# Own tiles for the last gate stores, the division in the score banks, and an output projection interleaved by row blocks

## The chip, the cores and the metric

The kernel runs on one core of a Trainium2 chip. The metric is the device time of one execution in microseconds (us); lower is better. A core has five instruction queues that run side by side and each in its own order: PE (TensorE, the matmuls), ACT (ScalarE), DVE (VectorE), POOL (GpSimd) and SP, which only issues DMAs here. An instruction that waits holds up everything behind it on its own queue.

## What is computed

The reference is one layer of a decoder: 1024 tokens and 16 learned meta tokens ahead of them, width 1024.

```python
h = rms_norm(h_res, pre_norm_g[i])
z = h @ w_in[i]                                   # 1024 -> 7328 columns
(pv, pg, cq, ckv, kr, mg, cu, cg, sbcx, sg, gl) = split_cols(z)
y_a = (pool_mixer(pv, ...) * silu(pg)) @ w_out_pool[i]
y_b = (mla_attention(cq, ckv, kr, ...) * silu(mg)) @ w_out_mla[i]     # 8 heads, causal
y_c = (conformer_conv(cu, ...) * silu(cg)) @ w_out_conf[i]
y_d = (short_conv(sbcx, ...) * silu(sg)) @ w_out_sc[i]
gts = sigmoid(gl + gate_bias[i]).reshape(b_, l_, 4, D_MODEL)
m = gts[:, :, 0] * y_a + gts[:, :, 1] * y_b + gts[:, :, 2] * y_c + gts[:, :, 3] * y_d
h_res = h_res + rms_norm(m @ w_o[i], post_norm_g[i])
return h_res[:, N_META:]
```

## The kernel before, in words

**Arithmetic.** Every large product is made of three matmuls: each fp32 operand is split into a rounded part and the rest (`split`: a copy on ACT, then a subtraction on POOL or DVE), and hi times hi, hi times lo and lo times hi are summed in PSUM. A matmul of 128 rows and 512 columns is the usual unit.

**Order of the work.** No instruction is written where it runs. The program's text records instructions (`Plan.record`), and `Plan.flush` plays them through a model: every instruction has a cost and becomes ready when what it depends on has ended, and each free engine takes the ready one of the lowest priority number. That order is then issued. `plan.ahead(n)` lowers the priority numbers, `plan.behind()` makes an instruction wait for the last matmul recorded. Tiles live in pools with a number of slots per tag; a tile of a tag gets the next slot that comes free, and two pools of different stages may lie over the same bytes. The real waits between engines and DMAs are semaphores put in afterwards from the true data dependences.

**Stage 1: input projection.** `unit` multiplies a 256-column pair of weight blocks with the normalised tokens by a seven-product scheme (A11, A12, A22 and the sums S1 to S4 of weight blocks against B11, B21, T1 to T4 and B22 of token blocks). It works in PSUM banks `ps_pa` to `ps_pd`, and calls `out(i, j, ...)` for the four 128 x 512 results in the order (1,1), (1,0), (0,0), (0,1). For the gates, `out_gate` adds on DVE, takes a tanh on ACT into a tile `z`, and stores it to DRAM (`th_dram`). The `z` tiles come from a tag with three slots (`halves_of`). Stores are issued on ACT's queue, and for the last pair of gates (g == 30) on POOL's. The seven split weight blocks of a pair are tiles of the tag `blk`, seven slots.

**Stage 2: attention.** For 8 heads and 2 halves of the queries, `attend` makes scores in PSUM (`ps_s`, tag `s`, five banks, taken as they come free), exponentiates them on ACT, splits the result (`pt`: ACT, then POOL) and multiplies with the values into `ps_o`. `maxima` runs ahead for the row maxima of the next unit and writes them into extra rows of the query tile `qt`. Between the units, `fills` computes the output products of the other three branches into `ps_y` (tag `y`, two banks): 48 products of six matmuls, each followed on DVE by a gate multiplication (`th`), and for the second and third of these branches by an addition into `m`: on POOL for the second, on DVE for the third. The division by the softmax sum goes through DRAM (`sums`) for the first seven heads, and for the last head through PE (`sums_pe`): four transposes of the sums, a reciprocal `lcp` on DVE, four transposes back, in two banks of the tag `y`.

**Stage 3: output projection.** First eight steps of the attention's own output product (`ps_u`), then `m @ w_o` by the same seven products, on 128-row blocks t = 0 to 3: `product(ps, b, name, t, ...)` is 12 matmuls (4 slices k of the weight, 3 each). The weights are loaded raw (`wr`, three slots) on SP's queue, four slices for each of the seven names, and split into tiles `wa` (ten slots), the low part on POOL for even k and on DVE for odd k. Row block t gives rows t and t + 4 of the output, four 512-column quarters: `c11` and `a_` for t, `u2` and `c22` for t + 4. Each quarter is squared on ACT with a running sum (`square`), multiplied by the norm's gain on POOL (`gain`), and `final(t, ...)` makes the reciprocal root (DVE, then a power on POOL, `rso`), scales and adds the residual rows `xr` on DVE (`scalar_tensor_tensor`) and stores on SP's queue. The last three products run in turn over all row blocks: S1 for t = 0..3 (`c22`), S4 for t = 0..3 (`u2`, rows t + 4 are finished), A22 for t = 0..3 (`a_`, rows t are finished). The last A22 product is done in two halves of 256 columns.

Of the kernel before, what the change touches and what calls it, by code (L numbers as in the profile page):

```python
# [21 lines left out]
F32 = mybir.dt.float32  # L22
# [8 lines left out]
P = 128  # L31
# [183 lines left out]
class Plan:  # L215
# [8 lines left out]
    def __init__(self, nc):  # L224
        self.nc, self.ops, self.todo, self.lift, self.pipe = nc, [], [], 0, None
        self.pools, self.past, self.extra, self.landed, self.wait = [], [], 0, [], None
# [57 lines left out]

    @contextmanager
    def slow(self, ns):

        self.extra += ns
        yield
        self.extra -= ns  # L290
# [26 lines left out]
    def record(self, eng, op, args, kw):  # L317
# [4 lines left out]
        if kw.get("accum_out") is not None:  # L322
# [4 lines left out]
            isinstance(v, View) and v.buf.psum for v in outs + ins)  # L327
        o = {"i": len(self.ops), "turns": turns, "prio": len(self.ops) - self.lift, "eng": eng, "op": op, "args": args, "kw": kw,
             "cost": cost, "bytes": nbytes, "extra": 0 if getattr(getattr(outs[0], "buf", None), "dram", True) else self.extra, "bufs": set(), "deps": set() if self.wait is None else {self.wait}, "users": [], "end": None}
# [26 lines left out]
    def flush(self):  # L356
# [38 lines left out]
        while events:  # L395
# [11 lines left out]
            for e in self.free:  # L407
# [21 lines left out]
                self.free[e] = t + o["cost"]  # L429
                o["end"] = t + o["cost"] + self.WAKE[e]  # L430
                if o["op"] == "dma_start":
# [28 lines left out]
def trunk_kernel(ctx, tc, a):  # L460
# [285 lines left out]
    def out_gate(g):  # L746

        def each(i, to, ps, x, tmp):
            if x is not None:
                full(to, x, ps)  # L750
            ACT.activation(to, ps if x is None else to, AF.Tanh, scale=0.5,
                           bias=par[:, R_GB + g + i:R_GB + g + i + 1])
        return halves_of(512, each, lambda i, j, t: (POOL if g == 30 else ACT).dma_start(half(th_dram[g + i], j), t))

# [746 lines left out]
    def sums_pe(h, c):  # L1501

        pc = bank("y")[:, :256].rearrange("p (j n) -> p j n", n=64)
        for j in range(4):
            PE.transpose(pc[:, j].in_order(), ol[h][64:, c, P * j:P * (j + 1)], ident[64:, 64:])
        lc = at.tile([P, 4], F32, tag="lcp", bufs=2, name="lcp")
        DVE.reciprocal(lc, pc[:, :, 0])
        rb = bank("y")[:64]
        for j in range(4):
            PE.transpose(rb[:, P * j:P * (j + 1)], lc[:, j:j + 1].to_broadcast([P, 64]), ident)  # L1510
        return rb
# [22 lines left out]
    def fills():  # L1534
# [9 lines left out]
        for bi, (gi, wname, b0) in enumerate(branches):  # L1544
            bo = [bos[bi, k] for k in range(2)]
            for d in range(KD):
# [8 lines left out]
                for c in range(2):  # L1555
# [128 lines left out]
    def weights(name):  # L1684

        for k in range(KH):
# [56 lines left out]

    def gain(src, i, out=None, c0=0):

        n = src.shape[1]
        mul(POOL, src if out is None else out, src, pgB[:, 512 * i + c0:512 * i + c0 + n])

    AHEAD = 60

    def final(t, h0, h1):

        rs_ = slice(P * t, P * (t + 1))
        with plan.ahead(AHEAD):
            DVE.tensor_reduce(rso[:, t:t + 1], sso[:, t], axis=AX.X, op=ALU.add)

            rsqrt_mean(rso[:, t:t + 1], rso[:, t:t + 1], D, 16 * EPS)
        for i, h in enumerate((h0, h1)):
            s_ = slice(512 * i, 512 * (i + 1))
# [38 lines left out]
    for t in range(4):  # L1798
        po[t], c22[t] = bank("o"), half("c22")
# [4 lines left out]
    for t in range(4):  # L1804
        product(po[t], B22, "S4", t, False, True)
        add(DVE, u2[t], po[t], u2[t])
        square(t + 4, 0, u2[t])
        gain(u2[t], 0)
        final(t + 4, u2[t], c22[t])
    for t in range(4):  # L1810

        parts = [slice(0, 512)] if t < 3 else [slice(0, 256), slice(256, 512)]
        g = half("g", 1) if t == 3 else a_[t]
        for i, cols in enumerate(parts):
# [4 lines left out]
            square(t, 1 + i, a_[t][:, cols])  # L1819
            gain(a_[t][:, cols], 1, g[:, cols], cols.start)  # L1820
        final(t, c11[t], g)
    plan.hold(kept, -1)
# [36 lines left out]
```

## Time and profile before

| | us |
|---|---|
| runs | 983.56, 987.5, 989.2 (median 987.5) |
| the profiled execution, its own time | 983.37 |
| its span, first to last instruction | 981.2 |
| PE busy in the span | 961.4 (98%) |
| DVE, POOL, ACT busy | 689.3, 679.2, 449.1 |
| mean granted TensorE clock | 0.991 |

Between the span and the execution's own time lie 2.2 us. In the trace all instructions of the body have the line L354, since the plan issues all of them there; so they are told apart by tile names (`ps_s<-qt,kt`: a score product) and by time. Stage 1 runs to 641.2 us, stage 2 to 851.6, stage 3 to the end. In a timeline row the first number is the start and the second the duration, "x12" counts merged instructions, and the bracket at the end gives the idle time of that engine just before and what ended it. PEq, ACTq and the like are an engine's queue; a row "SPq ... DMA" is the issue of a DMA, not its transfer.

### The profile page before, as it was taken

Reading aid. Unit: us, or ns where it says so; the run is one execution under the profiler, and the core shown is the slowest. Engines: PE = TensorE matmul, PEld = TensorE weight load, DVE = VectorE, ACT = ScalarE, POOL = GpSimd, SP = SyncE. Lnnn points to the kernel's source line nnn. Section 1 sums busy time; section 2 is a strip of 40 time slices with the busy share of each in tenths; the row PEclk is TensorE's granted clock in tenths of the full one; section 3 lists DMA queues with packets and bytes.
Section 4 is the critical chain, followed back from the end, with each engine's and each line's share of the span. In section 5 each row is a group of like instructions: output and inputs, shape, how many; then the busy total and the mean of one; then the engine's idle time right before and its main releaser. Section 6 shows DMA issues by size and latency. Waiting matters only on the chain.

```text
span 981.2 us, 15371 instructions
## 1 busy us (share of the span) xinstructions
PE 961.4 (98%) x5063; PEld 819.9 (84%) x5063; DVE 689.3 (70%) x1109; ACT 449.1 (46%) x914; POOL 679.2 (69%) x632
## 2 busy tenths in 40 slices
PE   9999999999999999999999999979999999999996
PEld 9999899889888888888788888868788888788885
DVE  6946968968969965445554777236867778699747
ACT  7644333343343554544443444356465565224631
POOL 6747645666677797877687789346387896546956
PEclk9999999999999999999999999979999999999998
DMA  7146567667686687675746788679859764772534
GB/s 255 35 114 174 154 223 231 199 213 255 195 279 232 200 260 213 220 245 181 210 153 191 235 292 279 174 238 330 224 165 289 196 196 130 257 253 92 188 123 172
DMA packets 136295, 202.76 MB, mean 207 GB/s; under 512 B 20814, under 2 KB 83253, under 8 KB 135448
## 3 DMA queue, kind: packets, MB, share of 16 engines
q1 hardware_dynamic: 127240, 185.00, 60.9%
q10 hardware_dynamic: 8656, 15.74, 4.4%
q0 software_dynamic: 320, 1.05, 0.3%
q8 instruction: 40, 0.66, 0.3%
q14 instruction: 39, 0.32, 0.1%
HBM read 128.86 MB, written 72.88 MB: 206 GB/s over the span
## 4 chain that ended last, share of the span: by engine, by line
PE 91%; DVE 4%; DMA 3%; issue 1%; ACT 1%; SPq 0%; POOL 0%; DVEq 0%; POOLq 0%; ACTq 0%
PE ps_pb L354 16%; PE ps_pa L354 16%; PE ps_pc L354 15%; PE ps_o L354 9%; PE ps_pd L354 7%; PE ps_u L354 7%; PE ps_s L354 7%; PE ps_y L354 6%; PE ps_x L354 5%; PE ps_w L354 1%; DMA th<-z 1%; DMA kt<-k 1%; DMA vt<-v 1%; DVE th L354 1%; DVE a L354 1%
## 5 line engine op out<-in xcount | busy, mean ns | idle before, releaser
L354 PE MATMUL ps_pb<-T,S 128*128 128x512 f32 (+2 forms) x792 | 172.4, 360 | 0.0
L354 PE MATMUL ps_pa<-B,A 128*128 128x512 f32 (+2 forms) x792 | 169.4, 359 | 0.0
L354 POOL TENSOR_TENSOR S<-ss,S 128x512 fp32r<-128x512 f32 x84 | 114.0, 1369 | 62.1 <-ACT S L354 61.9
L354 PEld LDWEIGHTS ps_pa<-B,A 128*128 128x128 f32 x792 | 134.3, 188 | 22.5 <-issue 0.7
L354 PEld LDWEIGHTS ps_pb<-T,S 128*128 128x128 f32 x792 | 134.1, 189 | 22.4 <-issue 1.0
L354 POOL TENSOR_TENSOR A<-raw,A 128x512 fp32r<-128x512 f32 x84 | 114.7, 1371 | 43.4 <-ACT A L354 37.0
L354 POOL TENSOR_TENSOR pt<-p,pt 128x512 fp32r<-128x512 f32 (+1 forms) x96 | 101.5, 1080 | 44.1 <-PE ps_s L354 22.7
L354 DVE TENSOR_TENSOR u<-ps_pb,u 128x512 f32<-128x512 f32 (+2 forms) x66 | 40.2, 610 | 80.6 <-PE ps_pb L354 76.7
L354 DVE SCALAR_TENSOR_TENSOR ps_w<-conv,par,ps_w 128x512 f32<-128x512 f32 x116 | 87.2, 752 | 2.3
L354 ACT ACTIVATE S<-ss 128x512 fp32r<-128x512 f32 x84 | 50.8, 628 | 81.5 <-DVE ss L354 50.1
L354 PE MATMUL ps_pc<-B,S 128*128 128x512 f32 (+1 forms) x396 | 86.2, 360 | 0.0
L354 PE MATMUL ps_pd<-T,A 128*128 128x512 f32 (+2 forms) x396 | 85.4, 359 | 0.0
L354 PE MATMUL ps_y<-bo,whl 128*128 128x512 f32 x288 | 85.1, 404 | 0.2 <-DVE th L354 0.2
L354 PE MATMUL ps_pc<-T,S 128*128 128x512 f32 (+1 forms) x396 | 85.0, 358 | 0.0
L354 PEld LDWEIGHTS ps_pc<-B,S 128*128 128x128 f32 x396 | 66.9, 189 | 11.7 <-issue 1.2
L354 PEld LDWEIGHTS ps_pc<-T,S 128*128 128x128 f32 x396 | 66.9, 189 | 10.7
L354 ACT ACTIVATE p<-ps_s 128x512 f32<-128x512 f32 (+4 forms) x112 | 49.4, 442 | 57.8 <-PE ps_s L354 31.3
L354 PE MATMUL ps_s<-qt,kt 100*128 100x512 f32 (+4 forms) x336 | 70.8, 334 | 5.1 <-DVE qt L354 5.1
L354 PEld LDWEIGHTS ps_pd<-T,A 128*128 128x128 f32 x396 | 66.9, 189 | 10.4
L354 PE MATMUL ps_o<-pt,vt 128*128 128x512 f32 (+7 forms) x288 | 68.3, 347 | 1.4 <-ACT ol L354 1.3
L354 DVE TENSOR_TENSOR z<-ps_pc,u 128x512 f32<-128x512 f32 (+1 forms) x66 | 40.2, 609 | 41.0 <-PE ps_pc L354 29.0
L354 PEld LDWEIGHTS ps_s<-qt,kt 100*128 100x128 f32 (+1 forms) x336 | 55.9, 183 | 15.1 <-DVE qt L354 5.4
(275 smaller groups left out, 1916.7 us busy)
## 6 DMA issues: line engine op xcount, KB each, us to landing
raw<-in_w_in_dram SPq DMA_DIRECT2D x52, 512.0 KB
th<-th SPq DMA_DIRECT2D x32, 512.0 KB
th<-z ACTq DMA_DIRECT2D x60, 256.0 KB
v<-vhl SPq DMA_DIRECT2D x16, 384.0 KB
qt<-q SPq DMA_DIRECT2D x16, 384.0 KB
vt<-v SPq DMA_DIRECT2D x8, 768.0 KB
bo<-bo SPq DMA_DIRECT2D x6, 1024.0 KB
kt<-k SPq DMA_DIRECT2D x8, 520.0 KB
```

The source lines that it names most:

```text
L354: getattr(self.handle[o["eng"]], o["op"])(*map(real, o["args"]), **{k: real(v) for k, v in o["kw"].items()})
```

## The change

Four edits, all in where tiles live and in what order work is recorded:

1. The last pair of gates (g == 30) writes its two output blocks into two tiles `zlast` of 1024 columns in the tag `blk`, instead of four `z` tiles. The stores stay on POOL's queue.
2. `sums_pe` takes its two PSUM banks from the tag `s` instead of `y`, and the plan counts 700 ns more until the reciprocal's result can be used (`plan.late`; it adds no instruction).
3. In `fills`, the additions of the second branch go to DVE for the first half of the columns (c == 0) and stay on POOL for the other half: 8 of 16 move.
4. The output projection's last three products (S1, S4, A22) are recorded row block by row block in the order below. Each block's rows are finished as soon as they are there. `wa` gets twelve slots, and two slices of A22 go into slots of the tag `th`; `c22` moves to slots of the tag `whl`; the residual rows are loaded in the order 0, 4, 1, 5, 2, 6, 3, 7. For the last block, the gain of the first 256 columns moves to DVE, and that of the second is recorded after the root.

```diff
@@ out_gate
-        return halves_of(512, each, lambda i, j, t: (POOL if g == 30 else ACT).dma_start(half(th_dram[g + i], j), t))
+        if g < 30:
+            return halves_of(512, each, lambda i, j, t: ACT.dma_start(half(th_dram[g + i], j), t))
+        zs = {}
+
+        def last(i, j, ps, x, tmp):
+            if i not in zs:
+                zs[i] = wp.tile([P, 2 * 512], F32, tag="blk", bufs=7, name="zlast")
+            z = half(zs[i], j)
+            each(i, z, ps, x, tmp)
+            POOL.dma_start(half(th_dram[g + i], j), z)
+        return last
@@ sums_pe
-        pc = bank("y")[:, :256].rearrange("p (j n) -> p j n", n=64)
+        pc = bank("s")[:, :256].rearrange("p (j n) -> p j n", n=64)
...
-        DVE.reciprocal(lc, pc[:, :, 0])
-        rb = bank("y")[:64]
+        with plan.late(700):
+            DVE.reciprocal(lc, pc[:, :, 0])
+        rb = bank("s")[:64]
@@ fills
-                        add(POOL if bi == 1 else DVE, m_[c][d], m_[c][d], t)
+                        add(POOL if bi == 1 and c else DVE, m_[c][d], m_[c][d], t)
@@ weights
-            t = wa[name, k] = ep.tile([P, 2, 512], F32R, tag="wa", bufs=10, name="wa")
+            tag, n = ("th", 3) if name == "A22" and k % 2 == 0 else ("wa", 12)
+            t = wa[name, k] = ep.tile([P, 2, 512], F32R, tag=tag, bufs=n, name="wa")
@@ end of the output projection
-    for i, t in enumerate((4, 5, 6, 7, 0, 1, 2, 3)):
+    for i, t in enumerate((0, 4, 1, 5, 2, 6, 3, 7)):
...
+            if i < len(parts) - 1 or t < 3:
+                gain(a_[t][:, cols], 1, g[:, cols], cols.start, DVE if t == 3 else POOL)
+        final(t, c11[t], g, (lambda: gain(a_[t][:, cols], 1, g[:, cols], cols.start, POOL)) if t == 3 else None)
+
+    ends = slice(0, 256), slice(256, 512)
+    for name_, t in (("S1", 0), ("S1", 1), ("S4", 0), ("A22", 0), ("S1", 2), ("S4", 1), ("A22", 1), ("S1", 3), ("S4", 2), ("A22", 2), ("S4", 3)):
+        {"S1": right, "S4": left, "A22": upper}[name_](t)
+    upper(3, ends)
```

**On DVE at the seam of stages 1 and 2.** These are the last instructions of stage 1 and the first of stage 2, with the semaphores each waits for (DMASW0 is a DMA issued on POOL's queue, DMAHW one issued on SP's or ACT's); `z` and `zlast` are gate results, `qt` the query tile. Before:

```order
L354 TENSOR_TENSOR u_6707<-ps_pb,u_6707 128x512 [waits DVE_49,PE_49]
L354 TENSOR_TENSOR z<-ps_pc,u_6707 128x512 [waits DMAHW7_49,DVE_49]
L354 TENSOR_TENSOR z<-ps_pd,u_6707 128x512 [waits DMAHW1_49,DMAHW0_49,PE_49]
L354 TENSOR_TENSOR z<-ps_pc,u_6722 128x512 [waits DMASW0_49,PE_49,Activation_49]
L354 TENSOR_TENSOR qt<-ps_s,ident 4x512 [waits DMAHW2_49,PE_49]
```

And now:

```order
L362 TENSOR_TENSOR u_6707<-ps_pb,u_6707 128x512 [waits DVE_49,PE_49]
L362 TENSOR_TENSOR zlast<-ps_pc,u_6707 128x512 [waits DVE_49]
L362 TENSOR_TENSOR zlast<-ps_pd,u_6707 128x512 [waits PE_49]
L362 TENSOR_TENSOR zlast<-ps_pc,u_6722 128x512 [waits PE_49]
L362 TENSOR_TENSOR qt<-ps_s,ident 4x512 [waits DMAHW2_49,PE_49]
```

The order is the same; the three additions of the last gates wait for PE or DVE alone now, and for no DMA. The wait for these stores has moved to SP's queue, where two loads in stage 2, `whl` and `th` for the second and third row of fills, now carry DMASW waits and stand behind the value tile `vt` of the third head.

**On PE at the end of stage 2.** `ps_y<-bo,whl` are fills, `ps_o<-pt,vt` and `pz,vs` the attention's value products, `ident,ol` and `ident,lcp` the transposes of `sums_pe`, `ps_u` is the start of stage 3. Before:

```order
L354 MATMUL ps_y<-bo,whl 128x512 x7
L354 MATMUL ps_o<-pz_6944,vs_6903 128x16
L354 MATMUL ps_y<-bo,whl 128x512 x8
L354 MATMUL ps_y<-ident,ol 128x64 x4
L354 MATMUL ps_y<-ident,lcp 64x128 x4
L354 MATMUL ps_y<-bo,whl 128x512 x18
L354 MATMUL ps_y<-ident,ol 128x64 x4
L354 MATMUL ps_y<-ident,lcp 64x128 x4
L354 MATMUL ps_u<-boM_8050,whl 128x512 x3
```

And now, from the last value product on:

```order
L362 MATMUL ps_o<-pz_6942,vs_6901 128x16
L362 MATMUL ps_y<-bo,whl 128x512 x3
L362 MATMUL ps_s<-ident,ol 128x64 x4
L362 MATMUL ps_y<-bo,whl 128x512 x8
L362 MATMUL ps_s<-ident,lcp 64x128 x4
L362 MATMUL ps_y<-bo,whl 128x512 x13
L362 MATMUL ps_u<-boM_8030,whl 128x512 x3
```

Eight fill matmuls stand between the two groups of transposes of the second half. Those of the first half have moved ahead, to before the value products of that last unit, with eight value matmuls between them.

**On PE and DVE in the output projection.** `ps_o<-wa,mh` are S1 and S4 products (12 matmuls each), `ps_u<-wa,B` are A22 products, each B a slice k of T4. PE before, from the end of S3 on:

```order
L354 MATMUL ps_o<-wa,mh 128x512 x96
L354 MATMUL ps_u<-wa,B_10253 128x512 x3
L354 MATMUL ps_u<-wa,B_10260 128x512 x3
L354 MATMUL ps_u<-wa,B_10273 128x512 x3
L354 MATMUL ps_u<-wa,B_10279 128x512 x3
```

PE now:

```order
L362 MATMUL ps_o<-wa,mh 128x512 x36
L362 MATMUL ps_u<-wa,B_10256 128x512 x3
L362 MATMUL ps_u<-wa,B_10261 128x512 x3
L362 MATMUL ps_u<-wa,B_10269 128x512
L362 MATMUL ps_o<-wa,mh 128x512 x5
L362 MATMUL ps_u<-wa,B_10269 128x512 x2
L362 MATMUL ps_u<-wa,B_10275 128x512 x3
L362 MATMUL ps_o<-wa,mh 128x512 x19
```

The first A22 product stood behind 96 matmuls and stands behind 36 now; five matmuls of the third S1 product stand inside it. DVE's last instructions before (`g` and `a` are the quarters of A22, `rso` the root; a `SCALAR_TENSOR_TENSOR` scales a quarter and adds the residual):

```order
L354 TENSOR_TENSOR a<-ps_o,a 128x256
L354 SCALAR_TENSOR_TENSOR c_10123<-c_10123,rso,xr 128x512
L354 SCALAR_TENSOR_TENSOR a<-a,rso,xr 128x512
L354 TENSOR_REDUCE rso<-sso 128x1
L354 TENSOR_SCALAR rso<-rso 128x1
L354 SCALAR_TENSOR_TENSOR c_10144<-c_10144,rso,xr 128x512
L354 SCALAR_TENSOR_TENSOR a<-a,rso,xr 128x512
L354 SCALAR_TENSOR_TENSOR c_10181<-c_10181,rso,xr 128x512
L354 SCALAR_TENSOR_TENSOR g<-g,rso,xr 128x512
```

And now:

```order
L362 TENSOR_TENSOR a<-ps_o,a 128x256
L362 SCALAR_TENSOR_TENSOR a<-a,rso,xr 128x512
L362 TENSOR_REDUCE rso<-sso 128x1
L362 TENSOR_SCALAR rso<-rso 128x1
L362 SCALAR_TENSOR_TENSOR u_10280<-u_10280,rso,xr 128x512
L362 SCALAR_TENSOR_TENSOR c_10539<-c_10539,rso,xr 128x512
L362 TENSOR_TENSOR g<-a,pgB 128x256
L362 SCALAR_TENSOR_TENSOR c_10176<-c_10176,rso,xr 128x512
L362 SCALAR_TENSOR_TENSOR g<-g,rso,xr 128x512
```

After the last eviction from PSUM (`a<-ps_o`) one scale-and-add stands ahead of the last root's first step where two stood; behind it stand four, and a 256-column gain, where four stood. On POOL the last two gains of 256 columns stood together ahead of the last power; now one does.

More of the change, by code (lines that the diff above doesn't have):

```diff
@@ L225, in __init__ @@
         self.nc, self.ops, self.todo, self.lift, self.pipe = nc, [], [], 0, None
+        self.after = 0
         self.pools, self.past, self.extra, self.landed, self.wait = [], [], 0, [], None
@@ L285, in slow, with late @@
     @contextmanager
+    def late(self, ns):
+        self.after = ns
+        yield
+        self.after = 0
+    @contextmanager
     def slow(self, ns):
@@ L327, in record @@
             isinstance(v, View) and v.buf.psum for v in outs + ins)
-        o = {"i": len(self.ops), "turns": turns, "prio": len(self.ops) - self.lift, "eng": eng, "op": op, "args": args, "kw": kw,
+        o = {"i": len(self.ops), "late": self.after, "turns": turns, "prio": len(self.ops) - self.lift, "eng": eng, "op": op, "args": args, "kw": kw,
              "cost": cost, "bytes": nbytes, "extra": 0 if getattr(getattr(outs[0], "buf", None), "dram", True) else self.extra, "bufs": set(), "deps": set() if self.wait is None else {self.wait}, "users": [], "end": None}
@@ L429, in flush @@
                 self.free[e] = t + o["cost"]
-                o["end"] = t + o["cost"] + self.WAKE[e]
+                o["end"] = t + o["cost"] + self.WAKE[e] + o["late"]
                 if o["op"] == "dma_start":
@@ L1742, in square, with gain, final @@
         ACT.activation(half("junk", 1)[:, :src.shape[1]], src, AF.Square, accum_out=sso[:, t, i:i + 1])
-    def gain(src, i, out=None, c0=0):
+    def gain(src, i, out=None, c0=0, eng=POOL):
         n = src.shape[1]
-        mul(POOL, src if out is None else out, src, pgB[:, 512 * i + c0:512 * i + c0 + n])
+        mul(eng, src if out is None else out, src, pgB[:, 512 * i + c0:512 * i + c0 + n])
     AHEAD = 60
-    def final(t, h0, h1):
+    def final(t, h0, h1, more=None):
         rs_ = slice(P * t, P * (t + 1))
@@ L1757, in final @@
             rsqrt_mean(rso[:, t:t + 1], rso[:, t:t + 1], D, 16 * EPS)
+        if more:
+            more()
         for i, h in enumerate((h0, h1)):
@@ L1793, in trunk_kernel, with right @@
         later(T4, k)
-    for i, t in enumerate((4, 5, 6, 7, 0, 1, 2, 3)):
+    for i, t in enumerate((0, 4, 1, 5, 2, 6, 3, 7)):
         xr[t] = cp.tile([P, D], F32, tag=f"m{(0, 1, 0, 1, 2, 3, 2, 3)[i]}{(1, 1, 0, 0, 1, 1, 0, 0)[i]}", name="xr")
         ld(xr[t], a["x"][0, P * t:P * (t + 1), :])
-    for t in range(4):
-        po[t], c22[t] = bank("o"), half("c22")
+    def right(t):
+        po[t], c22[t] = bank("o"), ep.tile([P, 512], F32, tag="whl", bufs=5, name="c22")
         product(po[t], T1, "S1", t, True, True)
@@ L1803, in trunk_kernel, with left, upper @@
         gain(c22[t], 1)
[L1804 to L1808, printed above, removed]
+    def left(t, parts=(slice(0, 512),)):
+        for i, cols in enumerate(parts):
+            product(po[t][:, cols], B22, "S4", t, False, True, cols)
+            with plan.ahead(AHEAD):
+                add(DVE, u2[t][:, cols], po[t][:, cols], u2[t][:, cols])
+            square(t + 4, (0, 2)[i], u2[t][:, cols])
+            gain(u2[t][:, cols], 0, None, cols.start)
         final(t + 4, u2[t], c22[t])
-    for t in range(4):
-        parts = [slice(0, 512)] if t < 3 else [slice(0, 256), slice(256, 512)]
-        g = half("g", 1) if t == 3 else a_[t]
+    def upper(t, parts=(slice(0, 512),)):
+        g = half("g", 1) if len(parts) > 1 else a_[t]
         for i, cols in enumerate(parts):
@@ L1819, in trunk_kernel @@
             square(t, 1 + i, a_[t][:, cols])
-            gain(a_[t][:, cols], 1, g[:, cols], cols.start)
-        final(t, c11[t], g)
+            if i < len(parts) - 1 or t < 3:
[5 more added lines that the diff above has]
+    upper(3, ends)
     plan.hold(kept, -1)
```

## The prediction, made before the changed kernel had run

> **What bounds the kernel now.** I read the page first: busy time, the clock by slice, the chain that ended last.
>
> ```profile
> PE 961.4 (98%) x5063; PEld 819.9 (84%) x5063; DVE 689.3 (70%) x1109; ACT 449.1 (46%) x914; POOL 679.2 (69%) x632
> PEclk9999999999999999999999999979999999999998
> PE 91%; DVE 4%; DMA 3%; issue 1%; ACT 1%; SPq 0%; POOL 0%; DVEq 0%; POOLq 0%; ACTq 0%
> ```
>
> PE is busy for 961.4 of 981.2 us and holds 91% of the chain, and no matmul goes away. So time can be won only in the 19.8 us in which PE stands still, and where its clock is low: one slice reads 7, at about 640 us, the seam of stages 1 and 2. Next come the timelines of PE, DVE and POOL there and at the end, and the chain in order of time (the last row).
>
> ```profile
> 640.80 0.38 PE L354 MATMUL ps_s<-ident,mrs 128*4 128x128 f32 x2
> 646.31 3.94 PE L354 MATMUL ps_s<-qt,kt 100*128 100x512 f32 x15 [5.13 <-DVE qt L354]
> ...
> 970.11 1.60 PE L354 MATMUL ps_o<-wa,B 128*128 128x256 f32 x12
> ...
> 622.02 0.69 DVE L354 TENSOR_TENSOR z<-ps_pc,u 128x512 f32<-128x512 f32 x1 [4.80 <-PE ps_pc L354]
> 644.85 0.69 DVE L354 TENSOR_TENSOR z<-ps_pc,u 128x512 f32<-128x512 f32 x1 [8.60 <-DMA th<-z]
> 645.57 1.28 DVE L354 TENSOR_TENSOR qt<-ps_s,ident 4x512 fp32r<-4x512 f32 x2
> ...
> 635.32 0.76 POOL L354 DMA_DIRECT2D th<-z  x1 [11.35 <-ACT z L354]
> ...
> 635.32 9.41 DMA th<-z
> ```
>
> PE idles 5.13 us for `qt`, which stands on DVE behind the last gate addition, and that one waits for a slot: the fourth `z` tile needs the slot of the first, whose store on POOL's queue took 9.41 us. The windows show what the pause does to the clock (columns: stretch, length, PE busy, granted clock, DMA share, GB/s).
>
> ```profile
> 643.00:643.50 0.50, 0.00 (x0) 0.87 0.98 398
> 643.50:644.00 0.50, 0.00 (x0) 0.50 1.13 449
> 653.00:654.00 1.00, 1.00 (x5) 0.70 0.99 360
> 974.00:974.50 0.50, 0.00 (x0) 0.96 0.93 348
> ```
>
> At 643.4, 2.2 us after PE's last matmul, the clock falls to half, and it is whole again only at about 653.6; after the kernel's last matmul (971.7) it fell at 974.5, 2.8 us later.
>
> **The change part by part.** *Gates in own tiles: the pause.* The last addition now waits for PE alone. Row 622.02 is such an addition, 0.1 us after its matmuls; those end at 640.9 here. So it starts at 641.0, `qt` 0.72 later (as 644.85 to 645.57), PE 0.74 after that (645.57 to 646.31): 642.5 instead of 646.3, **-3.8 us**, and 1.3 us of pause stay. Late next would be the first heads' loads, which the trace shows landed only in so far as PE runs at 646.3; were they the wait, the term would be anything down to 0. The wait for the stores goes to SP's queue, where `whl` and `th` now stand for it with all loads behind them:
>
> ```profile
> 663.51 0.43 SPq L354 DMA_DIRECT2D whl<-w_out_pool  x1
> ```
>
> SP came there at 663.5. The last store is issued at about 642.5 and at 9.4 us lands by 652: covered, price 0, and it would cost PE whatever a store took beyond some 15 us.
>
> *The clock.* A pause of 1.3 us is shorter than the 2.2 after which it fell. From 646.3 to 653.6 PE ran 7.3 us at half rate, 3.65 us of work: the upper bound. Not all is won, as the first value products wait for the scores' way through ACT and POOL:
>
> ```profile
> 648.37 0.60 ACT L354 ACTIVATE p<-ps_s 128x512 f32<-128x512 f32 x1 [2.08 <-DVE ps_s L354]
> 649.72 2.99 POOL L354 TENSOR_TENSOR pt<-p,pt 128x512 fp32r<-128x512 f32 x3 [2.30 <-ACT pt L354]
> 653.02 1.07 PE L354 MATMUL ps_o<-pt,vt 128*128 128x512 f32 x3
> ```
>
> ACT began 2.06 us after PE's first score, whose three matmuls take 0.64 us less at full rate: 1.42. POOL follows 1.35 later (648.37 to 649.72), its first piece (512 of 1184 columns in 2.99 us) takes 1.3, so the low part is there at 4.1, and the value products that needed it came 6.7 us after the first score before. That is 2.6, and 0.2 for the rest of the slow stretch: **-2.8 us** (0 to -3.65). The Trainium skill, "TensorE: Matmul & The Clock Gate", Part 1, says that the array goes to half rate after an idle window of about 3.4 us and back after about 3.4 us of activity. By it the slow stretch would cost 1.7 us; the trace shows 7.3 us of half rate, so the row decides.
>
> *The division in the score banks.* PE at the end of stage 2:
>
> ```profile
> 844.18 0.46 PE L354 MATMUL ps_y<-ident,ol 64*128 64x64 f32 x4 [0.32 <-DVE th L354]
> 845.60 0.62 PE L354 MATMUL ps_y<-ident,lcp 128*64 128x128 f32 x4 [0.96 <-DVE lcp L354]
> 851.21 0.62 PE L354 MATMUL ps_y<-ident,lcp 128*64 128x128 f32 x4 [0.48 <-DVE lcp L354]
> ```
>
> The three waits are 1.76 us. Eight matmuls, some 1.8 us, now stand between the transposes of each half, more than the 0.96 and 0.48 that the reciprocal was late; the 0.32 for a bank may stay. **-1.4 us** (0 to -1.8; a later `th` addition on DVE could take its place).
>
> *Eight additions from POOL to DVE.* The columns here are busy us of PE, PEld, DVE, ACT and POOL, then clock and DMA; below, DVE's addition beside a POOL operation and alone.
>
> ```profile
> 750.00:800.00 50.00, 49.16 (x261) 41.13 (x260) 38.33 (x95) 28.57 (x66) 44.69 (x44) 1.00 0.77 217
> ...
> 842.06 1.47 DVE L354 TENSOR_TENSOR m<-m,th 128x512 f32<-128x512 f32 x1
> ...
> 844.16 0.69 DVE L354 TENSOR_TENSOR m<-m,th 128x512 f32<-128x512 f32 x1
> ```
>
> Eight at 0.69 to 1.47 are 5.5 to 11.8 us on a DVE that is idle for 11.7 of 50, and POOL, the fuller one, is relieved. PE stands still 0.84 us in this window, so a gain ends there: **0** (-0.5 to +1.5, if DVE's evictions come late).
>
> *Interleaving: the weights.* Rows of PE, SP, ACT and DVE:
>
> ```profile
> 938.76 21.92 PE L354 MATMUL ps_o<-wa,mh 128*128 128x512 f32 x96
> 960.52 9.76 PE L354 MATMUL ps_u<-wa,B 128*128 128x512 f32 x48
> ...
> 917.24 4.55 SPq L354 DMA_DIRECT2D wr<-so  x2
> 937.55 8.61 SPq L354 DMA_DIRECT2D wr<-in_w_o_dram  x4
> ...
> 904.32 1.31 ACT L354 ACTIVATE wa<-wr 128x512 fp32r<-128x512 f32 x2
> ...
> 953.16 0.68 DVE L354 TENSOR_TENSOR wa<-wr,wa 128x512 fp32r<-128x512 f32 x1
> ```
>
> 96 matmuls take 21.76 us (to 960.52), a product of 12 takes 2.72. The first A22 product came at 960.52 and comes after three products now, at 946.9; by the new order its fourth slice is needed 14 matmuls (3.2 us) later, at 950.1. Before, that slice was split by 953.8: at the old pace PE would wait **3.7 us**. But slices follow each other at (945.8 - 917.24) / 11 = 2.6 us, and the two splits at 904.32 had waited for `wa` slots; with two slots more, and two A22 slices in `th` slots, the row of slices is two ahead, 5.2 us: 948.6, with 1.5 us to spare. I take **+0.4 us** (0 to 3.7).
>
> *Interleaving: the end.* DVE, POOL and SP after PE's end at 971.7:
>
> ```profile
> 972.82 0.41 DVE L354 TENSOR_TENSOR a<-ps_o,a 128x256 f32<-128x256 f32 x1
> 974.94 0.14 DVE L354 TENSOR_REDUCE rso<-sso 128x1 f32<-128x4 f32 x1
> 977.39 0.74 DVE L354 SCALAR_TENSOR_TENSOR g<-g,rso,xr 128x512 f32<-128x512 f32 x1
> ...
> 973.27 2.33 POOL L354 TENSOR_TENSOR g<-a,pgB 128x256 f32<-128x256 f32 x2
> 975.56 0.99 POOL L354 TENSOR_TENSOR rso<-rso,mhalf 128x1 f32<-128x1 f32 x1
> ...
> 978.20 0.33 SPq L354 DMA_DIRECT2D out_dram<-g  x1
> ```
>
> The last eviction is 1.1 us late, since eight row blocks were finished back to back on DVE; then come two scalings, the root (at 3.2 us after PE's end), two gains on POOL (2.33) ahead of the power, and the last scaling ends at 6.4. Now two S1 products lie among the eight that finish blocks and only four of the eight run back to back at the end, so DVE is nearly level: eviction at 0.25, one scaling, root at 1.4, one gain on POOL, power done by 3.4; on DVE two scalings to 3.2, the gain of 256 (0.4), two scalings to 5.0. **-1.4 us** (-0.5 to -2.2).
>
> *Sum:* -3.8 - 2.8 - 1.4 + 0 + 0.4 - 1.4 = -9.0. Against the profiled execution's own 983.4 that is 974.4; that execution lies 4.1 under the median of the runs, so I forecast 987.5 - 9.0 = **978.5**.
>
> **The rivals.** *The loads take over at the seam (0.08).* The DMA engines are full until about 646:
>
> ```profile
> 640.00:645.00 5.00, 1.18 (x7) 0.63 (x5) 0.15 (x1) 0.00 (x0) 0.00 (x0) 0.84 1.04 307
> ...
> 625.57 0.54 SPq L354 DMA_DIRECT2D kt<-k  x1
> ...
> 628.91 5.40 DMA vt<-v
> ```
>
> If `qt` or `kt` of the first heads land last, PE starts at 645.8 and the clock falls all the same: the seam gives 0.5 of 6.6 us, the time is 984.6. Against it: the first `kt` was issued ahead of `vt`, and that landed at 634.3.
>
> *The weights are late (0.13).* At the old pace PE waits 3.7 us at the first A22 product, beyond the 2.2 at which the clock fell, and up to 3.65 us of half rate follow: -9.4 + 3.7 = -5.7 to -2.1, 981.8 to 985.4. For it: ACT, POOL and DVE split in queues behind evictions. Against: before, the last slice was there 6.7 us ahead of the product.
>
> *DVE and POOL hold each other up (0.06).* Beside a POOL operation the addition took 1.47 us, alone 0.69. If the moved additions and the moved gain all meet one, the additions cost PE 1.5 us and the end 1.2: -9.0 + 2.7 = -6.3, 981.2. The Trainium skill, "SBUF — State Buffer", section "Who interferes with whom", speaks against this part of the change: a DVE instruction with two inputs in SBUF is blocked by a GpSimd instruction that reads SBUF until that one ends. By that the two rows agree.
>
> *Slower: the weights come later than before (0.03).* One mechanism at the same place: if POOL, with no gap in its queue, brings the fourth slice after 955.9, the pause is over 5.8 us, with 3.65 of half rate it eats the 9.4; at 8 us the time is 989.8. Against it: more slots can only bring the loads forward, and the order of SP's residual loads ahead of S4's slices is as before.
>
> That the change does not do what it says, because `zlast` waits for its own slot, costs nothing: the slot is that of A11's block, whose last product lies before 633.
>
> **How the numbers follow.** About 0.5% (4.9 us) is what a measurement of this kernel can tell from no change. My forecast has 0.70; its own range, with the ends of the terms, is -12 to -6.5: 975.5 to 981. The runs of before lie up to 3.9 under their median, so the low end gets 2 us more: 973.5. The high end reaches into the first two rivals: 984.5. Faster by over 0.5% means under 982.6: the forecast, the port rival and a quarter of the late weights, 0.70 + 0.06 + 0.03 = 0.79. Within: 0.08 + 0.10 = 0.18. Slower: 0.03.
>
> **What would show it.** Right: a DVE `zlast` at about 641.0, PE's first score at 642.5, no half clock in 640 to 655, the same matmul of the stage some 6.6 us earlier; no wait over 0.3 us at `ident,lcp`; S1 to A22 without a pause on PE; the last store issued 5.1 us after PE's end. Wrong: a wait on `kt` or `qt` loads at the seam, a clock under 1.00 behind a shorter pause, a wait of PE for `wa` near the first A22 product, or a gap at the seam of stages 2 and 3 in place of those before it.

## The result, and the profile after

The changed kernel takes 974.63 us (median of 5 runs, 973.6 to 979.32); runs of the kernel before beside them took 983.4 to 992.07. The ratio is 0.9892, 95% interval 0.9851 to 0.9933: 1.1% faster. The profiled execution took 973.71 us with a span of 971.8, where the forecast for it was 974.4.

The page of the changed kernel, busy time, clock by slice and the chain that ended last:

```profile
PE 959.1 (99%) x5063; PEld 817.5 (84%) x5063; DVE 695.7 (72%) x1118; ACT 450.7 (46%) x914; POOL 672.1 (69%) x623
PEclk9999999999999999999999999999999999999999
PE 93%; DMA 2%; DVE 2%; POOL 2%; issue 1%; ACT 1%; DVEq 0%; SPq 0%; POOLq 0%; ACTq 0%
```

The slice that read 7 is a 9. PE stands still for 12.7 us instead of 19.8. PE's timeline of the changed kernel, at the seam of stages 1 and 2, at the end of stage 2 and at the end:

```profile
640.92 0.38 PE L362 MATMUL ps_s<-ident,mrs 128*4 128x128 f32 x2
642.58 2.27 PE L362 MATMUL ps_s<-qt,kt 100*128 100x512 f32 x15 [1.28 <-DVE qt L362]
645.27 0.49 PE L362 MATMUL ps_o<-pt,vt 128*128 128x512 f32 x1 [0.26 <-ACT pt L362]
...
649.26 0.22 PE L362 MATMUL ps_o<-pz,vs 80*128 80x16 f32 x1
...
836.51 0.96 PE L362 MATMUL ps_y<-bo,whl 128*128 128x512 f32 x3 [0.19 <-DVE th L362]
...
843.43 6.74 PE L362 MATMUL ps_u<-boM,whl 128*128 128x512 f32 x29
...
961.83 1.60 PE L362 MATMUL ps_o<-wa,B 128*128 128x256 f32 x12
```

The same two matmuls in the kernel before, the first `pz,vs` and the first of stage 3:

```profile
655.63 0.22 PE L354 MATMUL ps_o<-pz,vs 80*128 80x16 f32 x1
851.59 0.71 PE L354 MATMUL ps_u<-boM,whl 128*128 128x512 f32 x2
```

The differences add up to the whole. The first score comes 3.73 us earlier (646.31 to 642.58); the first `pz,vs` 6.37, so 2.64 more, which is the clock; stage 3 starts 8.16 earlier, so the rest of stage 2 gave 1.79; PE ends 8.27 earlier (971.70 to 963.43), so stage 3 gave 0.11; and the span is 9.40 shorter, so the way from PE's end to the last instruction gave 1.13.

The stores at the end, on SP, of the changed kernel, and ahead of them its last DVE work:

```profile
968.78 0.33 SPq L362 DMA_DIRECT2D out_dram<-g  x1
```

```profile
962.37 1.66 DVE L362 SCALAR_TENSOR_TENSOR c<-c,rso,xr 128x512 f32<-128x512 f32 x1
...
964.20 0.41 DVE L362 TENSOR_TENSOR a<-ps_o,a 128x256 f32<-128x256 f32 x1
```

The last store is issued 5.35 us after PE's end (6.50 before), and the last eviction still comes 0.77 late, behind a scaling that took 1.66 us beside POOL's gain (962.18 to 963.48), where most others take 0.74.

### The profile page after: what moved, and what is told of

Read it like the earlier page. It is cut to its first block, busy times and chain, and to the rows that moved or that the text cites. A ratio compares the mean times of both kernels' runs of the same rounds, so it can differ in the third digit from the quotient of the medians.

```text
span 971.8 us, 15351 instructions
## 1 busy us (share of the span) xinstructions
PE 959.1 (99%) x5063; PEld 817.5 (84%) x5063; DVE 695.7 (72%) x1118; ACT 450.7 (46%) x914; POOL 672.1 (69%) x623
## 3 DMA queue, kind: packets, MB, share of 16 engines
q0 software_dynamic: 320, 1.05, 0.3%
## 4 chain that ended last, share of the span: by engine, by line
PE 93%; DMA 2%; DVE 2%; POOL 2%; issue 1%; ACT 1%; DVEq 0%; SPq 0%; POOLq 0%; ACTq 0%
PE ps_pb L362 17%; PE ps_pa L362 16%; PE ps_pc L362 15%; PE ps_o L362 9%; PE ps_u L362 8%; PE ps_pd L362 7%; PE ps_y L362 7%; PE ps_s L362 7%; PE ps_x L362 5%; PE ps_w L362 1%; DMA kt<-k 1%; POOL pt L362 1%; DMA kt<-kr 1%; POOL boM L362 0%; ACT pt L362 0%
## 5 line engine op out<-in xcount | busy, mean ns | idle before, releaser
L362 PE MATMUL ps_s<-qt,kt 100*128 100x512 f32 (+4 forms) x336 | 68.0, 325 | 1.3 <-DVE qt L362 1.3
```

What stands on the lines that cost most here:

```text
L362: getattr(self.handle[o["eng"]], o["op"])(*map(real, o["args"]), **{k: real(v) for k, v in o["kw"].items()})
```

## The experiments

Twelve kernels, each timed against the kernel before on the same chip; figures in brackets are 95% intervals of the ratio. The changed kernel's own ratio, 0.9892, is from another batch of only five runs, so its interval (0.9851 to 0.9933) is the widest, and comparisons with it are loose. My theory was the prediction's: pause and clock at the seam bring 6.4 us, the division and the end 1 to 2 each, and the moved additions nothing. The main rival: the parts do not add up, because another engine takes over.

### One part alone

Own gate tiles alone, in the kernel before:

```diff
-        return halves_of(512, each, lambda i, j, t: (POOL if g == 30 else ACT).dma_start(half(th_dram[g + i], j), t))
...
+                zs[i] = wp.tile([P, 2 * 512], F32, tag="blk", bufs=7, name="zlast")
...
+            POOL.dma_start(half(th_dram[g + i], j), z)
```

> The kernel before with the own gate tiles alone. Theory (slot wait, then clock): the last gate addition starts at 641.1, PE's first score at 642.6 instead of 646.3 (-3.7), no stretch at half clock behind it (-2.6), so all of stage 2 is 6.4 us earlier; the waits of the transposes at the end of stage 2 (1.8 us) and the 6.5 us from PE's end to the last store stay: 983.4 - 6.4 = 977.0, ratio 0.9935. Rival (the clock falls all the same, and the rest of the gain is the other order that the plan gives stage 2): -3.7, ratio 0.996. Rival (loads bound the seam): first score after 644, less than -2.

Measured: 0.9971 (0.9955 to 0.9987). The seam did what was expected: first score at 642.39, no half clock there. But less than half of the 6.4 us arrived. PE's waits for `ol` in this run (in all, times, longest; the kernel before had 1.3 us), and PE's timeline where the longest stands:

```profile
PE ps_o L354 <- ACT ol L354: 3.7, 3, 2.2
```

```profile
802.22 4.74 PE L354 MATMUL ps_o<-pt,vt 128*128 128x512 f32 x13 [2.16 <-ACT ol L354]
```

Following it back, on ACT, on DVE and on POOL of this run:

```profile
801.57 0.60 ACT L354 ACTIVATE ol<-ps_o 128x512 f32<-128x512 f32 x1 [1.98 <-DVE op L354]
```

```profile
798.00 2.93 DVE L354 TENSOR_TENSOR op<-ol,rb 64x512 f32<-64x512 f32 x1
```

```profile
794.13 5.03 POOL L354 TENSOR_TENSOR pt<-p,pt 128x512 fp32r<-128x512 f32 x4
799.12 1.27 POOL L354 TENSOR_TENSOR m<-m,th 128x512 f32<-128x512 f32 x1
```

PE waits for the bank that ACT empties into `ol`, and ACT waits for DVE's two products with the old `ol`. Such a product takes 0.68 us when alone. Here the first takes 2.93 and ends at 800.93, 0.54 us after POOL's second-branch addition (800.39), which followed the `pt` operations without a gap. POOL was busy for 29.69 of the 30 us from 770 to 800. After this pause of 2.16 us the clock fell for one stretch of 3.4 us, too. The 2.4 us more of these waits and up to 1.7 us for the stretch at half clock cover the 3.5 us that are missing. This is the place for the moved additions.

The division in the score banks alone:

```diff
-        pc = bank("y")[:, :256].rearrange("p (j n) -> p j n", n=64)
+        pc = bank("s")[:, :256].rearrange("p (j n) -> p j n", n=64)
...
-        DVE.reciprocal(lc, pc[:, :, 0])
-        rb = bank("y")[:64]
+        with plan.late(700):
+            DVE.reciprocal(lc, pc[:, :, 0])
+        rb = bank("s")[:64]
```

> The kernel before with the division in the score banks alone. Theory: the three waits of 0.32, 0.96 and 0.48 us go, all else in place: -1.8 us, at least -1.4, ratio 0.9982. Rival (the 1.8 us that stages 2 and 3 gained beyond the clock are the moved additions and the other order): these waits go but as many come back at the fills, 0, ratio 1.000.

Measured: 0.9987 (0.9972 to 1.0003). The waits for `lcp` are gone; in the profiled execution one of 1.73 us for `mxs` stands at 813 us in their place, and the clock fell for one stretch behind it. That fits the rival as well as the theory, and the time does not separate them.

The moved additions alone:

```diff
-                        add(POOL if bi == 1 else DVE, m_[c][d], m_[c][d], t)
+                        add(POOL if bi == 1 and c else DVE, m_[c][d], m_[c][d], t)
```

> The kernel before with the eight additions moved to DVE alone. Theory: PE waits no less at ps_y and ps_o between 750 and 850 us, sum of these waits within 0.5 us of the 2.8 of before: 0, ratio 1.000. Rival (POOL was late for the value products): waits for ACT ol of 0.48 and 0.84 and for DVE th go, up to -1.5, ratio 0.9985. Rival (port): DVE additions near 1.5 us each and waits for DVE th or mxs of 1.5 us more, ratio 1.0015.

Measured: 0.9999 (0.9987 to 1.0011). As expected, nothing.

The end alone (slots of `wa`, `c22` and A22, load order, interleaving, gains and root):

```diff
+            tag, n = ("th", 3) if name == "A22" and k % 2 == 0 else ("wa", 12)
...
+    for name_, t in (("S1", 0), ("S1", 1), ("S4", 0), ("A22", 0), ("S1", 2), ("S4", 1), ("A22", 1), ("S1", 3), ("S4", 2), ("A22", 2), ("S4", 3)):
+        {"S1": right, "S4": left, "A22": upper}[name_](t)
+    upper(3, ends)
```

> The kernel before with the interleaved end alone (slots, load order, gain and root with it). Theory: no wait of PE for the A22 weights, and the last store is issued 5.35 us after PE's end instead of 6.5: -1.1 us, ratio 0.9988. Rival (weights late): a wait of PE at the first A22 product of up to 3.7 us that the changed kernel hides only since its stage 2 ends earlier: +2.6, ratio 1.0026.

Measured: 0.9982 (0.9966 to 0.9998), with no wait of PE for the weights and the last store 5.51 us after PE's end. The theory holds.

The four parts alone add up to 0.6% (0.29, 0.13, 0.01, 0.18); together they bring 1.1%. The four intervals together are wide enough to cover this gap; if it is real, the rest is in the company of the parts, which the next two runs test.

### The additions in company

Gate tiles and additions together, in the kernel before (both diffs above):

> The kernel before with the own gate tiles and the moved additions, nothing else. Theory (the two work only together): waits for ol fall from 3.7 us in all to 0.6, no half clock in stage 2, the waits for lcp (1.4) stay: 983.4 - 3.7 - 2.6 - 0.3 = 976.8, ratio to before 0.9933, against 0.9971 with the gate tiles alone. Rival (the additions bring nothing): ratio 0.997 again, waits for ol of over 2 us.

Measured: 0.9925 (0.9905 to 0.9944), one wait of 0.6 for `ol`, and no half clock in stage 2. (The profiled execution, 980.52 us against a median of 978.13, has a wait of 1.89 for `mr` at 689.8.) The changed kernel without the additions:

```diff
-                        add(POOL if bi == 1 and c else DVE, m_[c][d], m_[c][d], t)
+                        add(POOL if bi == 1 else DVE, m_[c][d], m_[c][d], t)
```

> The changed kernel with the eight additions back on POOL. Theory (POOL is the bound of the later heads once PE no longer loses time at the seam): POOL busy over 9.5 of 10 us between 770 and 800, waits of PE for ol of over 1 us come up there (2.16 and 1.29 with the gate tiles alone), perhaps one stretch at half clock: 3 to 5 us longer than the changed kernel, ratio to before 0.992 to 0.995. Rival (the moved additions are worth nothing here either, and those waits came from the old division): no wait over 0.6 for ol, ratio 0.989.

Measured: 0.9937 (0.9914 to 0.9959), where the changed kernel has 0.9892. The same chain is back, on PE, DVE and POOL of this run:

```profile
803.52 5.91 PE L362 MATMUL ps_o<-pt,vt 128*128 128x512 f32 x13 [2.16 <-ACT ol L362]
```

```profile
799.27 3.56 DVE L362 TENSOR_TENSOR op<-ol,rb 64x512 f32<-64x512 f32 x2
```

```profile
795.40 5.06 POOL L362 TENSOR_TENSOR pt<-p,pt 128x512 fp32r<-128x512 f32 x4
800.39 1.30 POOL L362 TENSOR_TENSOR m<-m,th 128x512 f32<-128x512 f32 x1
```

Both ways round the additions are worth about 0.45% (0.9971 to 0.9925, 0.9937 to 0.9892), some 4.5 us, and alone they are worth nothing. By time only the first pair is clear, since the intervals of the second overlap; there the chain in the trace decides. The windows 770 to 800 show what they do (length, then busy PE, PEld, DVE, ACT, POOL), with the gate tiles alone and with both:

```profile
770.00:800.00 30.00, 29.57 (x158) 24.39 (x156) 21.72 (x49) 18.81 (x41) 29.69 (x28) 1.00 0.61 178
```

```profile
770.00:800.00 30.00, 29.03 (x147) 23.44 (x147) 25.20 (x56) 16.88 (x38) 23.31 (x22) 1.00 0.72 198
```

POOL gets gaps (23.31 of 30 instead of 29.69). With both, the first product of the same pair falls into one of them (POOL is idle from 798.29 to 799.51):

```profile
798.86 0.68 DVE L354 TENSOR_TENSOR op<-ol,rb 64x512 f32<-64x512 f32 x1
```

The second, beside POOL again, takes 1.44. The Trainium skill, "SBUF — State Buffer", section "Who interferes with whom", says that a DVE instruction with two SBUF inputs contends with a GpSimd instruction that reads SBUF. The trace agrees: the first product took 2.93 us beside a full POOL and ended 0.54 us after POOL's last operation, and 0.68 us in the gap. One thing stays open: with the moved additions the plan also has DVE do this pair ahead of the next row maxima (`mr`, at 804.05) instead of right behind them (`mr` at 797.91 with the tiles alone, 799.19 without the additions). The relief of POOL and the other order come together, and no run takes them apart.

The changed kernel without the own gate tiles:

```diff
-                zs[i] = wp.tile([P, 2 * 512], F32, tag="blk", bufs=7, name="zlast")
...
+        return halves_of(512, each, lambda i, j, t: (POOL if g == 30 else ACT).dma_start(half(th_dram[g + i], j), t))
```

> The changed kernel with the z tiles back for the last gates. Theory (pause and clock are worth 3.7 and 2.6 us in the company of the other edits): pause of 4.4 to 5.1 us, two or three stretches of 3.4 us at half clock, 974.6 + 6.4 = 981.0, ratio to before 0.9957. Rival (the own tiles are worth what they brought alone, 0.0029): ratio 0.992.

Measured: 0.9977 (0.9957 to 0.9998). PE and the windows at the seam of this run:

```profile
646.55 3.94 PE L362 MATMUL ps_s<-qt,kt 100*128 100x512 f32 x15 [4.67 <-DVE qt L362]
```

```profile
645.00:655.00 10.00, 8.45 (x27) 7.17 (x28) 3.82 (x10) 4.33 (x11) 3.93 (x9) 0.50 0.56 203
```

Pause and half clock are back. In company the tiles are worth about 0.85%, alone 0.29%; the expected 6.4 us (0.65%) lie within what the two intervals allow, and the rival's 0.992 lies outside this run's.

### The weights and the end

The changed kernel with ten slots for the weights, A22 among them:

```diff
-            tag, n = ("th", 3) if name == "A22" and k % 2 == 0 else ("wa", 12)
-            t = wa[name, k] = ep.tile([P, 2, 512], F32R, tag=tag, bufs=n, name="wa")
+            t = wa[name, k] = ep.tile([P, 2, 512], F32R, tag="wa", bufs=10, name="wa")
```

> The changed kernel with the old ten slots for the weights, A22's slices among them. Theory (the two slots and the two slices in th slots bring the weights forward): PE waits at the first or fourth A22 slice, 1 to 3.7 us, and more if the clock falls: 975 to 979 where the changed kernel has 974.6, ratio to before 0.990 to 0.994. Rival (the weights have time to spare with ten slots too): no wait of PE for wa, ratio 0.989.

Measured: 0.9962 (0.9946 to 0.9978), about 7 us above the changed kernel, and PE never waits for `wa`. ACT of this run, its last PE work, and its last store:

```profile
949.01 1.26 ACT L362 ACTIVATE wa<-wr 128x512 fp32r<-128x512 f32 x2 [6.76 <-issue]
```

```profile
963.12 1.60 PE L362 MATMUL ps_o<-wa,B 128*128 128x256 f32 x12
```

```profile
975.75 0.33 SPq L362 DMA_DIRECT2D out_dram<-g  x1
```

The theory was right that the slots are needed and wrong about who pays. The plan moves PE's matmuls around the late slices. But two splits of the weights stand at the head of ACT's queue, which is idle for 6.76 us ahead of them. The row names no releaser ("issue"), but the semaphores in the trace point to one: ACT waits there for a count of PE's among others, and the matmul of an S product that raises it ends at 948.93, 0.04 us before ACT goes on at 948.97, while the last load of weights was over by 941. So the splits most likely wait until PE is done with an older slice, whose slot they need. The evictions on DVE behind their second halves come late, six squares then run in one piece from 953.6 to 958.1, gains and scalings back up behind those, and the last store comes 11.0 us after PE's end instead of 5.35.

The changed kernel with both gains of the last block on POOL ahead of the root:

```diff
-            if i < len(parts) - 1 or t < 3:
-                gain(a_[t][:, cols], 1, g[:, cols], cols.start, DVE if t == 3 else POOL)
-        final(t, c11[t], g, (lambda: gain(a_[t][:, cols], 1, g[:, cols], cols.start, POOL)) if t == 3 else None)
+            gain(a_[t][:, cols], 1, g[:, cols], cols.start)
+        final(t, c11[t], g)
```

> The changed kernel with both gains of the last block on POOL and recorded ahead of the root, as before. Theory (this part is most of what the end won): the first half's gain, 1 us, stands ahead of other work on POOL, the last store is issued 5.8 to 6.2 us after PE's end instead of 5.35: +0.5 to +0.9 us. Rival (the end won by the interleaved order alone): within 0.2 us of 5.35.

Measured: 975.63 us (median), ratio 0.9920 (0.9896 to 0.9944), too wide to tell it from the changed kernel by time. PE's last work and SP's last store of this run:

```profile
973.55 1.60 PE L362 MATMUL ps_o<-wa,B 128*128 128x256 f32 x12
```

```profile
981.52 0.33 SPq L362 DMA_DIRECT2D out_dram<-g  x1
```

The last store is issued 6.37 us after PE's end, later than the theory's 5.8 to 6.2 and far from the rival's 5.35. In the profiles of the six kernels that have the split gains and the new slots it is 5.35, 5.36, 5.36, 5.51, 5.98 and 5.98; in six with the old end 6.48 to 6.50. The 5.98 are no other end: those kernels issue their last instructions in the order of the changed kernel. So 0.63 of the 1.02 us between 5.35 and 6.37 can be a difference between executions. The nearest pair is the run without the own gate tiles, where as here a scaling of 1.78 us beside POOL holds up the evictions:

```profile
971.35 1.60 PE L362 MATMUL ps_o<-wa,B 128*128 128x256 f32 x12
...
978.93 0.33 SPq L362 DMA_DIRECT2D out_dram<-g  x1
```

There it is 5.98, so the two gains are worth 0.39 us in that pair and at most 1.02. That they are most of the 1.13 that the end won is not shown. The profiled execution of this run was an odd one, 986.31 us against its median of 975.63, and shows what made this one longer:

```profile
690.88 0.32 PE L362 MATMUL ps_s<-kt,qt 96*128 96x144 f32 x1 [3.83 <-DMA kt<-k]
...
771.01 0.30 PE L362 MATMUL ps_s<-kt,qt 96*128 96x144 f32 x1 [1.56 <-DMA kt<-k]
...
786.50 4.84 PE L362 MATMUL ps_o<-pt,vt 128*128 128x512 f32 x13 [2.37 <-ACT ol L362]
```

Keys and queries were loaded late in stage 2, and a low clock followed (0.57 from 691 to 695). Whether the changed kernel's own longer executions (978.01 and 979.32) lose their time in this way, no profile shows.

### The seam

What is left of the pause, 1.28 us, is the way from the last gate addition over `qt`. To take it away, the first head's rows in `qt` were made in stage 1 and loaded:

```diff
@@ task_first (stage 1)
+            PE.transpose(pm[:4, :P], mrs[:, h, c], ident)
...
+            ld(rows_dram[c], rows.rearrange("p r n -> p (r n)"))
@@ load_q
+        if h < FIRST:
+            ld(qt[h, c][QK:NA, 0, :], rows_dram[c])
@@ maxima
-            mr = mrs[:, h, c]
-            for _ in range(4):
+            for _ in range(5):
                 yield
+            return
```

> The changed kernel, with the four extra rows of the first head's query tiles made in stage 1 and loaded from DRAM, so that PE's first score waits for loads alone and for nothing on DVE. Theory (DVE's way from the last gate addition to qt is what the seam still waits for, and the loads are in time): first score at 641.2 instead of 642.6, the value products 1.0 to 1.4 us earlier: 0.9 to 1.4 us off. Rival (the loads are as late as the chain of waits has it, landing at 641.8): first score after 641.9, at most 0.6 off.

Measured: 0.9989 (0.9975 to 1.0003), some 9.5 us above the changed kernel. PE of this run, then SP, then SP of the changed kernel:

```profile
641.71 2.15 PE L362 MATMUL ps_s<-qt,kt 100*128 100x512 f32 x15
645.24 0.47 PE L362 MATMUL ps_o<-pt,vt 128*128 128x512 f32 x1 [1.38 <-DMA vt<-v]
```

```profile
633.77 0.54 SPq L362 DMA_DIRECT2D kt<-k  x1
```

```profile
625.73 0.54 SPq L362 DMA_DIRECT2D kt<-k  x1
```

The pause is gone: the score follows the stage's last matmul at once. But the extra steps put stage 1's side work later, and the loads are issued 8 us later; then values, keys and queries are late (1.4, 1.4 and more), and the clock falls. The edit does not test the way over DVE cleanly; it shows that the loads have less than 8 us to spare. A second try, with the side work at a higher pace (the loads of the rows, moved behind the first keys and values, are left out of this cut):

```diff
-             ): 0.9,
+             ): 0.95,
```

> As the run with the rows made in stage 1, but with the side work of stage 1 at a slightly higher pace (0.95 steps a unit instead of 0.9) and the loads of the rows behind those of the first head's keys and values, so that the loads at the seam are issued about as early as in the changed kernel (first keys at 625.7, second at 632.2). Theory (there it was the late issue of the loads, 8 us, that cost): the first score follows the stage's last matmul with no pause, no wait for vt or kt over 0.3, 0.9 to 1.3 us off the changed kernel's 974.6, ratio to before 0.988. Rival (the loads have no time to spare once the pause is gone): waits for vt and kt of 1 us and more as there, ratio 0.989 or above.

Measured: 1.0251 (1.0221 to 1.0281). PE and SP of this run:

```profile
671.35 5.39 PE L362 MATMUL ps_s<-qt,kt 100*128 100x512 f32 x18 [28.83 <-DMA qt<-q]
```

```profile
646.81 0.32 SPq L362 DMA_DIRECT2D bo<-bohi  x1
...
658.79 0.55 SPq L362 DMA_DIRECT2D kt<-k  x1
```

The pace moved another lane's last stores, `bo`, to 646.81 and after, ahead of the first loads on SP's queue (the last of them was issued at 611.18 in the changed kernel), and the first keys were issued at 658.79. It failed, and tells only how much hangs on that queue.

The last stores on ACT's queue, in the kernel before:

```diff
-        (POOL if g == 30 else ACT).dma_start(half(th_dram[g + i], j), t)
+        ACT.dma_start(half(th_dram[g + i], j), t)
```

> The kernel before with the last four gate stores on ACT's queue instead of POOL's, z tiles as they were. Theory (the store is slow because the DMA engines are full with the first heads' loads, not because of POOL's queue): the fourth z addition again waits for a store of 8 to 9 us, pause of 4 us or more, ratio to before 0.999 to 1.000. Rival (POOL's queue makes it slow; the store before it on ACT's queue landed after 2.05 us): addition at 641.0, pause of 1.3 us, ratio 0.997 as with the gate tiles alone.

Measured: 1.0134 (1.0110 to 1.0158), which neither expected. DVE of this run, PE, and its chain of waits:

```profile
642.06 0.69 DVE L354 TENSOR_TENSOR z<-ps_pc,u 128x512 f32<-128x512 f32 x1 [4.80 <-PE ps_pc L354]
```

```profile
651.77 3.91 PE L354 MATMUL ps_s<-qt,kt 100*128 100x512 f32 x15 [9.58 <-DMA kt<-kr]
```

```profile
643.54 4.35 DMA th<-z
647.91 0.33 SPq L354
```

The fourth addition waits for PE alone: its store, issued at 636.05, had landed within 6.0 us, and the last one took 4.35. But SP's loads now wait for the stores on ACT's queue (SP waited 29.3 us in all for stores of `z`, 5.7 in the kernel before): the chain goes from the store of 643.54 to the keys' second part at 647.91, and PE stands still for 9.58 us. The windows of this run say what that does to the comparison:

```profile
626.60:638.00 11.40, 11.40 (x52) 9.43 (x51) 2.76 (x4) 1.43 (x2) 0.27 (x4) 1.00 0.08 29
```

With the loads held back, the DMA engines were nearly idle (share 0.08, where before had 1.03 to 1.05 from 630 to 642), so these stores were quick in empty engines. Whether POOL's queue or the full engines made the 9.41 us stays open. What the run shows is why these stores are better off ACT's queue: there they hold up the first heads' loads.

## Why the prediction was right, point by point

| term | forecast | in the rows of the profile |
|---|---|---|
| pause at the seam | -3.8 | -3.73 |
| half clock behind it | -2.8 | -2.64 |
| division, and additions | -1.4 and 0 | -1.79, the rest of stage 2 |
| weights | +0.4 | -0.11 |
| the end | -1.4 | -1.13 |
| sum | -9.0 | -9.40 |

**Pause.** Right in mechanism and size: `zlast` at 641.12, the score at 642.58, and the pause is 1.28 us in the changed kernel and in all five runs with own tiles and the old way of `qt` (gate tiles alone, with the additions, the changed kernel without them, ten slots, both gains on POOL). In these traces the second load of keys was issued 9.94 to 10.55 us ahead of the score; a pause that waited for it would not repeat to 0.01 us, so the rival of the loads is out here, although the chain of waits names a load of keys that lands at 641.80: DVE's addition ends at the same moment.

**Clock.** The size was right. The reason, that a pause of 1.3 us is shorter than the 2.2 after which it fell, was not the rule: with the gate tiles alone it fell after a pause of 2.16 in one place, with the division alone after one of 1.73, and in the run with the end alone only 4.9 us after the last matmul. The 2.2 was where the pause lay on the grid shown at the end of this document. That 1.28 is short enough, six traces show; the forecast's reason for it did not.

**Division.** The three waits are gone and 0.19 is left; alone it measured -1.3 us (0.9987), with an interval that reaches zero.

**Additions.** The step that failed: "PE stands still 0.84 us in this window, so a gain ends there". That window belonged to a kernel that had lost 6.4 us at the seam and whose plan gave stage 2 another order. With the tiles alone, POOL has hardly a gap between 770 and 800 (29.69 of 30 us busy), DVE's `op` is held up, and PE waits 3.7 us and loses clock. So the tiles alone brought 0.29% of the 0.67% that pause and clock were forecast at, and the additions, put at 0, hold 0.45% in company. The sum came out right because both were in the change; that is luck, not a right reading of the parts. The rival in which DVE and POOL hold each other up named a mechanism that the traces show and had its sign the wrong way round: the moved additions end it here (together with the plan's other order).

**Weights.** No wait, as forecast; the step "at the old pace PE would wait 3.7 us" named the wrong payer. Without the slots it is ACT's queue and then the end that pay, 5.7 us.

**The end.** The size was near, the working was not: "eviction at 0.25" came at 0.77, since a scaling beside POOL took 1.66; and of the 1.13 us the nearest pair of profiles gives 0.39 to the split of the last two gains; how the rest divides is open.

**The forecast time.** 978.5 against 974.63. I added the 4.1 us by which the profiled execution of before lay under its median of three runs; in 35 runs beside the single parts the median of before was 985.87, 2.5 above it, and the changed kernel's median lies only 0.92 above its profiled execution. That is 3.2 of the 3.9 us; the other 0.7 is the profile's 973.71 against the 974.4 worked out.

## What to carry to other kernels

Price an edit in the schedule that the other edits leave behind, not in the trace of before: an engine with 10% of slack there can be the bound once a pause upstream is gone, and an edit that measures as nothing alone may hold a good part of the gain. When a term is priced at 0 because something else stands still less, ask what happens to that something when the other terms arrive. And a late transfer need not stop the engine that uses it: look at what is queued behind the instruction that prepares it, and at the end of the kernel.

## What the runs showed of the hardware

**The clock falls and rises on a fixed grid of 3.41 us.** Rows of the windows for the slice in which the clock changes (the clock is the third number from the end). First and last fall in the kernel before, then in the run with the end alone:

```profile
643.25:643.50 0.25, 0.00 (x0) 0.00 (x0) 0.00 (x0) 0.00 (x0) 0.00 (x0) 0.74 1.04 422
974.25:974.50 0.25, 0.00 (x0) 0.00 (x0) 0.25 (x1) 0.00 (x0) 0.25 (x2) 0.92 0.82 303
```

```profile
645.75:646.00 0.25, 0.25 (x2) 0.20 (x2) 0.25 (x1) 0.00 (x0) 0.21 (x1) 0.92 0.35 139
973.50:973.75 0.25, 0.00 (x0) 0.00 (x0) 0.25 (x1) 0.00 (x0) 0.24 (x1) 0.78 0.00 0
```

A slice that reads 0.74 was at 1.00 for 48% of it, so before fell at 643.37 and at 974.46, 331.09 us apart, 97.0 times 3.413. The run with the end alone fell at 645.96 and 973.64: 327.68, 96.0 times. With the gate tiles alone it fell at 803.65 and 970.90: 167.25, 49.0 times. In all eleven traces that have more than one fall the distances are whole multiples, and within the kernels the clock also rises on this grid. Stretches at half rate were 10.25 us (before), 6.8 (the end alone) and 3.4 (gate tiles alone): three, two and one steps of the grid. Of the steps at full clock, each in which PE was busy for 1.43 us (42%) or less ended in a fall, and none in which it was busy for more than 1.99 (58%) did. Between these, the share alone does not decide. The gate tiles alone, the division alone, and the run with the rows made in stage 1:

```profile
800.24:803.65 3.41, 1.43 (x6) 1.10 (x7) 3.31 (x6) 0.97 (x2) 0.15 (x1) 1.00 0.62 190
```

```profile
639.48:642.90 3.42, 1.58 (x9) 0.95 (x7) 0.00 (x0) 0.00 (x0) 0.21 (x1) 1.00 1.05 216
```

```profile
651.16:654.57 3.41, 1.99 (x11) 1.40 (x11) 0.28 (x1) 2.13 (x4) 2.43 (x2) 1.00 1.04 279
```

The clock fell after 1.43 us and after 1.99, and not after 1.58 (46%). What else counts stays open; the ends of the matmuls in a trace are modelled, so these shares are rough. The pause of 1.28 leaves 2.13 (62%) in the worst place of the grid, and no fall followed it in any of the six traces that have it. The Trainium skill, "TensorE: Matmul & The Clock Gate", Part 1, says that the window is free-running and 3413 ns long; the trace agrees. It also gives the rule of thumb that gaps over some 3.4 us are to be avoided; here gaps of 2.16 and 1.73 us were enough.
